# Token scaling for expert dispatch: the 8-token input tile moves to the front, and five of six weight loads move to the load queue

## The chip, the core and the metric

The kernel runs on one core of a Trainium2 chip. The metric is the time of one execution on the device, in microseconds (us); lower is better. The median of six runs is given, and beside it one execution that the hardware profiler recorded.

## What is computed

Each of 16 x 1024 = 16,384 tokens has a row of 512 float32 values, and two expert weights. The output holds, for each token, its row times the first weight and its row times the second:

```python
batch, seq, hidden = x.shape            # 16, 1024, 512
k = expert_indices.shape[-1]            # 2
x_expanded = x[:, :, np.newaxis, :].repeat(k, axis=2)
weights = expert_weights[..., np.newaxis]
return (x_expanded * weights).astype(np.float32)
```

The expert indices are not used for any value. The kernel reads 33.55 MB of input and 0.13 MB of weights, and writes 67.11 MB.

## The kernel before

The 16,384 tokens are dealt to 128 partitions, 128 tokens for each. The list `groups` cuts these 128 into input tiles: five tiles of 24 tokens per partition, then one of 8. A tile of 24 is 48 KB in each partition and 6 MB in all; a tile of 8 is 16 KB and 2 MB. Within a group a partition holds tokens that follow one another in memory, so a tile's load is one contiguous piece per partition.

Three pools hold the data. `w_pool` has one tile with all weights, two per token. `x_pool` has two buffers for input tiles. `o_pool` has two buffers for output tiles, each of `TO` = 12 tokens: 48 KB in each partition, 6 MB in all. An input tile of 24 tokens so becomes two output tiles and two stores; one of 8 tokens becomes one output tile of 32 KB per partition and a store of 4 MB.

There are two queues for transfers. SyncE (SP, the profile's q1) issues the weight loads at the start (line 55), one for each group, and then all stores (line 106). ScalarE (ACT, the profile's q10) issues the input loads (line 76), and computes as well. Each engine works through its instructions in order.

The helper `load(i)` takes an input buffer and issues the load of tile i. Tiles 0 and 1 are loaded ahead of the main loop; the load of tile i + 2 is asked for when tile i's products have been written down, and waits until they are done. In the main loop each token of a tile gives two products of 512 values. Every third product (column `c` of the weights, `c % 3 == 2`) is ScalarE's (line 91), the others are VectorE's (line 97). After each 12 tokens, or at the tile's end, the store is issued.

The framework puts in the waits: a product waits for its input tile, for the weights of its own columns, and for the store that last used its output buffer; a store waits for the products of both engines; a load waits until the products that read its buffer are done. A wait is put on an instruction of the engine that needs it, and what is behind it on this engine waits as well. The framework also decides the order of each engine's instructions, which is close to the order of the source but not always the same: an instruction that stands later in the source can be placed ahead of another that does not depend on it.

Of the kernel before, what the change touches and what calls it, by code (L numbers as in the profile page):

```python
# [1 line left out]

# [4 lines left out]


@with_exitstack
def kernel(  # L10
    ctx: ExitStack,
    tc: tile.TileContext,
    x: bass.AP,
    expert_indices: bass.AP,
    expert_weights: bass.AP,
    out: bass.AP,
):
    nc = tc.nc

    batch, seq, hidden = x.shape  # L20
    k = expert_weights.shape[-1]
    P = nc.NUM_PARTITIONS
    ntok = batch * seq
    assert ntok % P == 0
    A_TOTAL = ntok // P

    f32 = mybir.dt.float32
    row = k * hidden
    TX = 24
    TO = 12  # L30


    groups = [[24], [24], [24], [24], [24], [8]]
    assert sum(sum(g) for g in groups) == A_TOTAL

    xf = x.rearrange("b s h -> (b s) h")
    of = out.rearrange("b s k h -> (b s) (k h)")
    wf = expert_weights.rearrange("b s k -> (b s) k")

    w_pool = ctx.enter_context(tc.tile_pool(name="w_pool", bufs=1))  # L40
    x_pool = ctx.enter_context(tc.tile_pool(name="x_pool", bufs=2))
    o_pool = ctx.enter_context(tc.tile_pool(name="o_pool", bufs=2))

    w_tile = w_pool.tile([P, A_TOTAL * k], f32)

    def rows(of_all, done, T):
        return of_all[done * P : (done + T) * P, :].rearrange(
            "(p a) n -> p (a n)", a=T
        )

    weights = []
    for group in groups:
        weights.append((sum(n for _, n in weights), sum(group)))
    for at, T in weights:
        nc.sync.dma_start(out=w_tile[:, at * k : (at + T) * k], in_=rows(wf, at, T))

    tiles = []
    done = 0
    for group in groups:
        T = sum(group)  # L60
        a0 = 0
        for n in group:
            tiles.append((done, T, a0, n))
            a0 += n
        done += T

    loaded = []

    def load(i):
        if i >= len(tiles):  # L70
            return
        done, T, a0, n = tiles[i]
        x_tile = x_pool.tile([P, TX * hidden], f32)
        cols = rows(xf, done, T)[:, a0 * hidden : (a0 + n) * hidden]
        for lo, hi in [(0, P)]:
            nc.scalar.dma_start(out=x_tile[lo:hi, : n * hidden], in_=cols[lo:hi, :])
        loaded.append(x_tile)

    for i in range(2):
        load(i)  # L80
    for i, (done, T, a0, n) in enumerate(tiles):
        x_tile = loaded[i]
        outr = rows(of, done, T)
        for t in range(n):
            if t % TO == 0:
                o_tile = o_pool.tile([P, TO * row], f32)
            for kk in range(k):
                c = (done + a0 + t) * k + kk
                o = t % TO * row + kk * hidden
                if c % 3 == 2:  # L90
                    nc.scalar.mul(  # L91
                        out=o_tile[:, o : o + hidden],
                        in_=x_tile[:, t * hidden : (t + 1) * hidden],
                        mul=w_tile[:, c : c + 1],
                    )
                    continue
                nc.vector.tensor_scalar(  # L97
                    out=o_tile[:, o : o + hidden],
                    in0=x_tile[:, t * hidden : (t + 1) * hidden],
                    scalar1=w_tile[:, c : c + 1],  # L100
                    scalar2=None,
                    op0=mybir.AluOpType.mult,
                )
            if (t + 1) % TO == 0 or t + 1 == n:
                at = t // TO * TO
                nc.sync.dma_start(  # L106
                    out=outr[:, (a0 + at) * row : (a0 + t + 1) * row],
                    in_=o_tile[:, : (t + 1 - at) * row],
                )
        load(i + 2)  # L110

# [1 line left out]
_INS = ['x', 'expert_indices', 'expert_weights']  # L113
_OUTS = [((16, 1024, 2, 512), 'float32')]


# [23 lines left out]
```

## Time and profile before

| | before |
|---|---|
| median of six runs | 240.81 us (240.47 to 241.04) |
| the profiled execution | 241.0 us |
| its span, first to last instruction | 239.3 us |
| VectorE (DVE) busy | 68.6 us, 171 products of 482 ns |
| ScalarE (ACT) busy | 54.5 us, 85 products of 708 ns and a table load |
| moved by DMA | 100.81 MB, mean 421 GB/s |
| store queue q1 | 65.1% of 16 engines' time |
| load queue q10 | 33.0% |
| first multiply | at 18.51 us |
| stores issued | from 25.02 to 218.81 us, 11 of them |

The 16 DMA engines serve both queues. A transfer of 128 partitions is cut into 128 packets, one for each partition, 8 for each DMA engine, and the trace records when each packet began and how long it took. A share in the table is the sum of the packets' times of a queue over 16 times the span. The span is shorter than the execution's time, since starting and ending the program lies outside it. Times in the views are counted from the start of the span.

VectorE's products start 0.402 us apart where nothing holds them, so the 16 of an output tile take 6.42 us; ScalarE's 8 take 5.01 us beside them. A row of "waits" gives who waited, for what, how long in all, how often, and the longest. The "chain that ended last" is followed back from the last instruction, at each step to what released it.

### The profile page before, as it was taken

Reading aid. Unit: us, or ns where it says so; the run is one execution under the profiler, and the core shown is the slowest. Engines: PE = TensorE matmul, PEld = TensorE weight load, DVE = VectorE, ACT = ScalarE, POOL = GpSimd, SP = SyncE. Lnnn points to the kernel's source line nnn. Section 1 sums busy time; section 2 is a strip of 40 time slices with the busy share of each in tenths; the row PEclk is TensorE's granted clock in tenths of the full one; section 3 lists DMA queues with packets and bytes.
Section 4 is the critical chain, followed back from the end, with each engine's and each line's share of the span. In section 5 each row is a group of like instructions: output and inputs, shape, how many; then the busy total and the mean of one; then the engine's idle time right before and its main releaser. Section 6 shows DMA issues by size and latency. Waiting matters only on the chain.

```text
span 239.3 us, 363 instructions
## 1 busy us (share of the span) xinstructions
DVE 68.6 (29%) x171; ACT 54.5 (23%) x86; POOL 0.2 (0%) x4
## 2 busy tenths in 40 slices
DVE  0009920000370910640064037002805506415000
ACT  0109700000340800620061035002505206213000
POOL 0000000000000000000000000000000000000000
DMA  7999999999999999999999999999999999999894
GB/s 267 462 446 412 412 373 419 485 411 419 460 435 411 437 452 419 411 476 411 427 460 427 403 444 461 411 403 485 419 405 460 408 457 452 403 403 493 383 438 192
DMA packets 3314, 100.81 MB, mean 421 GB/s; under 512 B 1136, under 2 KB 1136, under 8 KB 1136
## 3 DMA queue, kind: packets, MB, share of 16 engines
q1 hardware_dynamic: 2448, 67.24, 65.1%
q10 hardware_dynamic: 864, 33.55, 33.0%
q14 instruction: 2, 0.02, 0.0%
HBM read 33.69 MB, written 67.11 MB: 421 GB/s over the span
## 4 chain that ended last, share of the span: by engine, by line
DMA 60%; DVE 17%; issue 14%; DVEq 0%; SPq 0%
DMA out_dram<-o_tile 53%; DVE o_tile L97 17%; DMA x_tile<-in_x_dram 7%; DVEq L135 0%; DVEq L97 0%; SPq L106 0%
## 5 line engine op out<-in xcount | busy, mean ns | idle before, releaser
L97 DVE TENSOR_SCALAR o_tile<-x_tile,w_tile 128x512 f32<-128x512 f32 x171 | 68.6, 482 | 150.1 <-DMA out_dram<-o_tile 99.2
L91 ACT ACTIVATE o_tile<-x_tile,w_tile 128x512 f32<-128x512 f32 x85 | 53.2, 708 | 157.3 <-DMA out_dram<-o_tile 145.8
L91 ACT ACT_TABLE_LOAD x1 | 1.3, 1283 | 5.7 <-DMA w_tile<-in_expert_weights_dram 5.7
L124 POOL MEMSET const-bfloat16-1.0<- 128x1 bf16 x1 | 0.1, 101 | 0.0
L124 POOL MEMSET const-uint8-127<- 128x1 uint8 x1 | 0.1, 101 | 0.0
L124 POOL MEMSET const-float32-0.0<- 128x1 f32 x1 | 0.1, 98 | 0.2 <-issue 0.2
L124 POOL MEMSET const-float32-1.0<- 128x1 f32 x1 | 0.1, 98 | 0.0
## 6 DMA issues: line engine op xcount, KB each, us to landing
out_dram<-o_tile SPq DMA_DIRECT2D x10, 6144.0 KB, 35.5
x_tile<-in_x_dram ACTq DMA_DIRECT2D x5, 6144.0 KB, 33.2
out_dram<-o_tile SPq DMA_DIRECT2D x1, 4096.0 KB, 19.5
x_tile<-in_x_dram ACTq DMA_DIRECT2D x1, 2048.0 KB, 23.6
w_tile<-in_expert_weights_dram SPq DMA_DIRECT2D x5, 24.0 KB, 31.8
w_tile<-in_expert_weights_dram SPq DMA_DIRECT2D x1, 8.0 KB, 31.2
```

The source lines that it names most:

```text
L91: nc.scalar.mul(out=o_tile[:, o : o + hidden], in_=x_tile[:, t * hidden : (t + 1) * hidden], mul=w_tile[:, c : c + 1],)
L97: nc.vector.tensor_scalar(out=o_tile[:, o : o + hidden], in0=x_tile[:, t * hidden : (t + 1) * hidden], scalar1=w_tile[:, c : c + 1], scala ...
L124: nc = _bacc.Bacc("TRN2", target_bir_lowering=False, num_devices=1)
```

## The change

The list of groups begins with the 8-token tile, and the five of 24 come behind it. Only the weights of the first group are still loaded by SyncE, ahead of its stores. ScalarE issues the other five weight loads, between the load of the first input tile and that of the second. The number of products, stores and loads, and their sizes, are the same. The tile of 8 tokens and its 4 MB store are now the first and not the last.

```diff
-    groups = [[24], [24], [24], [24], [24], [8]]
+    groups = [[8], [24], [24], [24], [24], [24]]
...
-    for at, T in weights:
-        nc.sync.dma_start(out=w_tile[:, at * k : (at + T) * k], in_=rows(wf, at, T))
+
+    def load_weights(queue, part):
+        for at, T in part:
+            queue.dma_start(out=w_tile[:, at * k : (at + T) * k], in_=rows(wf, at, T))
+
+    load_weights(nc.sync, weights[:1])
...
-    for i in range(2):
-        load(i)
+    load(0)
+    load_weights(nc.scalar, weights[1:])
+    load(1)
```

In the changed kernel the lines are numbered a little higher: the weight loads are line 57, the input loads line 80, ScalarE's products line 96, VectorE's line 102 and the stores line 111. In the built order, ScalarE's instructions before were: two loads, the 16 products of the first tile, the third load, the products of the second tile. After, they are: the 8-token load, five weight loads, the second tile's load, the 5 products of the first tile, one product of the second tile, the third load, the other products of the second tile.

## The prediction

> **What bounds the kernel now.** I read the page's slices first, then the queues, the chain and the waits, the windows, and last the records of single packets in the trace.
>
> ```profile
> DMA  7999999999999999999999999999999999999894
> q1 hardware_dynamic: 2448, 67.24, 65.1%
> q10 hardware_dynamic: 864, 33.55, 33.0%
> ```
>
> The first line is the busy share of the 16 DMA engines in 40 slices of 6 us: it is at its top from the second slice to the last but two. The next two are the store queue (SP, q1) and the load queue (ACT, q10): together 98.1% of the span. Nothing else is near its limit: VectorE is busy 29% and ScalarE 23%.
>
> ```profile
> 0.72 17.77 DMA x_tile<-in_x_dram
> 18.51 6.44 DVE o_tile L97 x16
> 188.80 25.38 DMA out_dram<-o_tile
> DVE o_tile L97 <- DMA x_tile<-in_x_dram: 18.5, 1, 18.5
> ACT o_tile L91 <- DMA out_dram<-o_tile: 145.8, 9, 35.1
> ```
>
> The first three are pieces of the chain (start, length, what), the others rows of the waits. The multiplies stand idle for 18.5 us at the start, until the first input tile has landed, and after that they wait for stores to give back output buffers. Neither idle time is idle time of the transfers, as the windows show (length; DVE, ACT and POOL busy; clock; DMA share; GB/s):
>
> ```profile
> 5.40:29.70 24.30, 11.19 (x29) 11.20 (x17) 0.00 (x0) 1.00 0.98 422
> 29.70:32.30 2.60, 1.58 (x4) 0.00 (x0) 0.00 (x0) 1.00 1.03 304
> 34.20:63.50 29.30, 0.00 (x0) 0.00 (x0) 0.00 (x0) 1.00 1.00 431
> 218.80:235.90 17.10, 0.00 (x0) 0.00 (x0) 0.00 (x0) 1.00 1.00 432
> ```
>
> So the end is set by how much the transfers have to move and by what they lose, hardly by when a multiply runs. The packet records give the sum. A 48 KB packet takes 1.815 us, a 32 KB one 1.213 and a 16 KB one 0.611; every transfer of 128 partitions gives each engine 8 packets. Loads: five of 8 x 1.815 and one of 8 x 0.611, 77.5 us. Stores: ten of 8 x 1.815 and one of 8 x 1.213, 154.9 us. That is 232.4 us for each engine. The first packet starts at 1.72, the last ends at 238.0, the span is 239.3, and this execution took 241.0: 1.7 outside the span. The median shown is 240.81, so 0.2 comes off at the end.
>
> The loss beside the 232.4 is small and can be placed. Packets that took longer than their size's usual time add 0.58 us per engine in the first 5 us, 0.84 between 29 and 32.2 us, and 0.21 in all the rest. All sixteen packets of the second group are an engine's last packet of the second input tile, and right behind each come weight packets:
>
> ```profile
> DMA packets 544, 1.64 MB, mean 364 GB/s; under 512 B 512, under 2 KB 512, under 8 KB 512
> w_tile<-in_expert_weights_dram SPq DMA_DIRECT2D x5, 24.0 KB, 31.8
> ```
>
> The first line is of the stretch 29.7 to 34.2 us: 512 small packets. The second says that weights on the store queue take 31.8 us to land. The records show why: with both queues filled, an engine takes one packet of each in turn, so one weight packet goes out with every 1.8 us of input.
>
> **The change part by part.** *The small tile in front.* In the first trace the first multiply starts at 18.51. The tile's eight packets per engine now take 0.611 instead of 1.815, so it starts at 18.51 - 8 x 1.204 = 8.9 us. Its 16 products take 4.44 us (the row of the last, 8-token tile), the first store (4 MB) is issued at 13.4 and, with the 1.0 us from issue (0.72) to first packet (1.72), moves from 14.4. Before it was issued at 25.02 and moved from 32.6. That is 18 us earlier, but the engines were moving input then, which has to be moved anyway: bytes and packet sizes are the same, only in another order. Worth nothing by itself.
>
> *The large tile at the end.* The last store is 6 MB instead of 4. The three last stores run back to back. An output buffer comes back 0.5 us after its store has landed, its multiplies take 6.44, the issue 0.05 and the first packet 1.0: 8.0 us, under the 14.5 us of the other buffer's store, which covers it. The stretch from the last packet's end to the span's end stays 1.3 us. Nothing again; uncovered, it would cost 8.0 each time.
>
> *The load of the third tile.* The built order has one more move that the diff doesn't show. Before, ScalarE issued this load behind the last product of the first tile. Now it stands behind the first product of the second tile, which waits for that tile to land. Behind this wait stand the load itself and 7 more products. Does the load queue's gap show? The second tile starts per engine at about 9.6 (first tile landed at 8.5, and about 1.2 for the weights, below). Three packets go out by 15.0, the other five alternate with the first store: 5 x (1.815 + 1.213) = 15.1, so it lands at 30.1. Then 0.4 to the product, 0.7 for it, 1.0 for issue to packet: the third tile moves from 32.2. The first store has three packets left at 30.1, that is 3.6 us, to 33.7. Covered by 1.5 us. The next store follows at 30.5 + 6.44 + 1.05 = 38.0, while the load runs. Zero, with a thin cover; without it 2.1 us.
>
> Here a rule of the Trainium skill speaks against the change. "DMA: Bandwidth & Descriptors", section "Queues, rings and completion order", has an engine drain a whole packet, some 9 to 17 descriptors, of one queue before it turns to another. By that the first store's eight would go at one turn, be done before the tile lands, and the gap of 2.1 us would be open. The records here alternate one by one (20 and 20 large packets of the two queues between 35 and 40 us), so I go by the row.
>
> *The weights in the load queue.* Each of the five transfers is 8 packets per engine and one 4-byte packet that signals the end: 45. Before, 15 of them went out between input packets at 0.016 us, 0.24 in all; 30 went in one run at a pitch of 0.0117, 0.35; and the packet before that run was stretched by 0.84. Removed: 1.43 us. Now all 45 stand in one run between the first and second tile, with nothing on the other queue: 45 x 0.0117 = 0.53, plus a stretch that this trace doesn't show. Bounds: nothing, if reading ahead hides it as it hid the 15 (sum 0.53, change -0.9); in proportion to the run above, 0.84 x 45/30 = 1.26 (sum 1.79, +0.4); at the rate of the start, where 9 small packets stand beside a stretch of 0.58, 0.58/9 x 45 = 2.9 (sum 3.4, +2.0). I take 1.26, from the nearest row: a run of the same packets right behind input. ScalarE issues the five at about 0.45 us each, so the second load is issued at about 4 us, before the first tile has moved: no cost; uncovered it would be 5 x 0.45 = 2.3 us. The first weights stay alone on SP; they land before the first tile as now (the table load, released by them, starts at 5.75).
>
> The same page, "Anatomy of one DMA", gives a fixed cost of about 2.0 us for each DMA issued by GpSimd, and its rules call transfers under 64 KB mostly overhead. Five in a row at that price would be 10 us and the total 249. On one engine the records have the ends of three such transfers at 32.34, 32.44 and 32.54: 0.1 us apart, so they don't wait for one another.
>
> Sum: 241.0 + 0.4 = 241.4 in the frame of the profiled execution, 241.2 as a median.
>
> **The rivals.** *Cheap run.* The stretch vanishes: 240.8 - 0.9 = 239.9. For it: the 15 interleaved packets cost their 0.016 and no stretch. Against it: both runs of small packets in this trace stand beside stretched ones. Chance 0.2.
>
> *Dear run, slower.* The price per small packet at the start holds: 240.8 + 2.0 = 242.8. It decides when the last packets of the first tile, 0.611 us each, are too short to hide the reading of 45 small pieces which 1.815 us half hid. For it: the cover is a third as long. Against it: the stretch at the start may be the first access and not the weights. Chance 0.2.
>
> *Dry queue.* The third tile's load comes after the first store has run out; up to 2.1 us on all engines, 242.3 to 242.9. It decides when the store has at most one packet left as the tile lands, that is when it starts less than two input packets after the tile. Chance 0.08.
>
> *It does what an earlier start suggests.* The multiplies begin 9.6 us sooner, and all of it shows: 231.2. Against it: 232.4 us of packets, 1.7 before, 1.3 behind and 1.7 outside are 237.1 already. Chance 0.02.
>
> **How the numbers follow.** The forecast, 241.2, has 0.5; its own range is 240.4 to 241.9, from a stretch that stays at 0.84 whatever the number, less the 0.3 by which runs differ, to the sum and as much again. About 0.2% (0.48 us) is what can be told from no change, so 240.33 to 241.29 counts as the same. Faster: the cheap run nearly whole, the last rival and a little of the forecast, 0.22. Slower: the dear run, most of the dry queue and a quarter of the forecast, 0.38. The same: 0.40. The range for 8 in 10 goes from the cheap run's 239.8 to the dear one's 242.9.
>
> **What would show it.** Right: a DMA share of 1.0 from about 10 us on; first multiply near 8.9; first store issued near 13.4; stretched input packets around 7 to 9 us, with about 1.8 us between the last first-tile packet at its usual time and the first large one of the second; the third load issued at about 31 with no lower DMA share at 30 to 34. Wrong: a dip in the share at any later place, a last packet that ends more than 2 us from 238.4, or a stretch of the engines' last packets in another place.

## The result, and the profile after

| | before | after |
|---|---|---|
| median | 240.95 us (41 runs) | 242.29 us (19 runs) |
| ratio, with its 95% interval | | 1.0056 [1.0044, 1.0067] |
| the profiled execution | 241.0 us | 242.94 us, a second one 241.65 us |
| its span | 239.3 us | 241.3 us, the second 240.0 us |

The changed kernel is slower by 1.3 us, 0.56%. It scatters more: 241.2 to 243.56 us, against 240.47 to 241.96. The first profile of it lies 0.65 us above its median and the second as far below.

The page's busy slices of the 16 DMA engines and the two queues, after:

```profile
DMA  6999999999999999999999999999999999999991
...
q1 hardware_dynamic: 1728, 67.12, 64.3%
q10 hardware_dynamic: 1584, 33.68, 33.2%
```

The bound is the same: 97.5% of the span is packets. The load queue now has the weights' packets, 720 more. Pieces of the chain (start, length, what):

```profile
4.22 25.35 DMA x_tile<-in_x_dram
...
29.66 6.44 DVE o_tile L102 x16
...
36.15 34.26 DMA out_dram<-o_tile
```

and rows of the waits (who waited for what: us in total, times, longest):

```profile
ACT o_tile L96 <- DMA out_dram<-o_tile: 136.7, 9, 29.2
...
DVE o_tile L102 <- DMA x_tile<-in_x_dram: 25.2, 2, 16.0
```

Both engines wait for inputs twice now, 9.2 and 16.0 us on VectorE, and for stores as before. The chain runs through the second tile's load, which lands at 29.6, and then through the second store, issued at 36.15. The timeline (start, length, engine, line, what) shows what stands between the two:

```profile
9.18 4.45 DVE L102 TENSOR_SCALAR o_tile<-x_tile,w_tile 128x512 f32<-128x512 f32 x11 [9.18 <-DMA x_tile<-in_x_dram]
...
29.65 0.72 ACT L96 ACTIVATE o_tile<-x_tile,w_tile 128x512 f32<-128x512 f32 x1 [17.30 <-DMA x_tile<-in_x_dram]
29.73 0.33 ACTq L80 DMA_DIRECT2D x_tile<-in_x_dram  x1
...
36.25 5.01 ACT L96 ACTIVATE o_tile<-x_tile,w_tile 128x512 f32<-128x512 f32 x8 [1.59 <-DMA out_dram<-o_tile]
```

ScalarE's single product of the second tile waits 17.30 us for that tile, and the third load, behind it, goes out at 29.73. The last row says that the first store had landed by 36.25, at about the moment that the second was issued. So the store queue had nothing to move until then, and another 3.9 us pass from that issue to a first packet. The DMA view of 33.6 to 37.6 us (queue, kind: packets, MB, share) says it directly:

```profile
q10 hardware_dynamic: 33, 1.62, 93.9%
q1 hardware_dynamic: 6, 0.00, 0.1%
```

Six store-queue packets in 4 us, all of them 4-byte ends of a transfer. The packet records put the first store's last packets at 32.8 to 34.0 us and the second store's first ones at 40.1 to 41.8. On one engine that is a pause of 7.3 us between two store packets, in which it moves four load packets. The engines were not idle: the third load ran alone. The loss therefore has to be sought in the packets themselves. Time beyond the usual for a packet's size, in us per engine, in both profiles of each kernel (packets sorted by when they began):

| began at | before | before, second | after | after, second |
|---|---|---|---|---|
| 0 to 7 us | 0.58 | 0.46 | 0.44 | 0.51 |
| 7 to 33 us | 0.84 | 0.77 | 0.65 | 0.11 |
| 33 to 60 us | 0.00 | 0.00 | 0.47 | 0.73 |
| 60 us to the end | 0.21 | 0.18 | 0.36 | 0.07 |
| mean end of the 16 engines | 236.53 | 236.45 | 237.11 | 236.74 |
| last end | 238.01 | 238.11 | 239.94 | 238.66 |

The mean engine of the first profile ends 0.58 us later, the last one 1.93. The execution ends with the last. The row of 33 to 60 us is new: it is nothing before the change, and it begins where the store queue starts again. In the second profile a smaller second row makes up for it: summed over the whole execution the stretches are 1.63 and 1.41 us before, 1.92 and 1.42 after. What sets both profiles of the changed kernel apart is how unevenly the engines end: the last is 1.48 and 1.66 us behind the mean before, 2.83 and 1.92 after. The stretches of 33 to 60 us fall unevenly: two engines in the first profile and three in the second have load packets stretched one after the other, some 4 us apart, between 35 and 54 us. The records don't name an engine. I joined packets to chains by their times, and an engine's own share is less sure than the means and the last end.

### The profile page after: what moved, and what is told of

Read it like the earlier page. It is cut to its first block, busy times and chain, and to the rows that moved or that the text cites. A ratio compares the mean times of both kernels' runs of the same rounds, so it can differ in the third digit from the quotient of the medians.

```text
span 241.3 us, 364 instructions
## 1 busy us (share of the span) xinstructions
DVE 68.7 (28%) x171; ACT 54.6 (23%) x86; POOL 0.2 (0%) x4
## 4 chain that ended last, share of the span: by engine, by line
DMA 65%; DVE 16%; another core or an unknown queue 7%; ACTq 1%; issue 1%; DVEq 0%; SPq 0%
DMA out_dram<-o_tile 55%; DVE o_tile L102 16%; DMA x_tile<-in_x_dram 11%; ACTq L57 1%; ACTq L80 0%; DVEq L140 0%; DVEq L102 0%; SPq L111 0%
```

## The experiments

Each run has its own runs of the kernel before beside it on the same chip, and ratios are against these. Edits are shown against the changed kernel where nothing else is said. The first four take the change apart.

**Order alone** (all six weight loads on the store queue):

```diff
-    load_weights(nc.sync, weights[:1])
+    load_weights(nc.sync, weights)
...
-    load_weights(nc.scalar, weights[1:])
```

> The tiles are in the changed order (8 tokens in front), all six weight loads are on the store queue as before. Theory W (the five weight loads in the load queue cost the 1.35 us): back to 240.9 to 241.2, ratio 0.999 to 1.001. Theory O (the order: with the small tile in front the store queue runs empty once after its first store, at 33 to 40 us, and each start of stores stretches load packets): still slower, 241.9 to 242.7, ratio 1.004 to 1.007. Both: a stretched input packet per engine just ahead of its first store packet, 0.6 to 0.85 us on average, if the stretch belongs to the first store; if it belongs to runs of weight packets, it stands where those are.

240.84 us, ratio 0.9989 [0.9968, 1.0010]: not slower. It has the 8-token tile in front and the late third load (issued at 24.41). But the first store waits in its queue behind the weights, whose packets go out one for each input packet: it is issued at 13.49 and moves from 23 us. So it lasts to 38 or 41 us. The second store is issued at 30.84, so the store queue never runs out; 0.05 us of stretched packets at 33 to 60 us. Theory W foretold the time, and as the next but one shows for another reason.

**Weights alone** (the old order of tiles):

```diff
-    groups = [[8], [24], [24], [24], [24], [24]]
+    groups = [[24], [24], [24], [24], [24], [8]]
```

> The tiles are in the old order, the five later weight loads are in the load queue between the first two input tiles. Theory W: 241.9 to 242.7, ratio 1.004 to 1.007. Theory O: as before, 240.5 to 241.2, ratio 0.998 to 1.001. If the stretch of 0.84 us ahead of the first store belonged to the weights, it moves to about 17 us; if to the first store, it stays just ahead of the first store packet, which now can start sooner since nothing is queued before it on the store queue.

240.70 us, 0.9975 [0.9962, 0.9988]. Moving the weights costs nothing; Theory W is refuted here. The stretched packets begin at 26.7 to 31.6 us (0.60 in all), just ahead of the first store's first packets at 28.9 to 31.7, with no weight packet near: these went out from 17.0 to 18.7 us.

**The change without its five later weight loads:**

```diff
-    load_weights(nc.scalar, weights[1:])
...
-                        mul=w_tile[:, c : c + 1],
+                        mul=w_tile[:, c % 16 : c % 16 + 1],
```

(and the same column for VectorE's products)

> The changed kernel without its five later weight loads; all products use the first tile's weight columns, so the output is not the reference's. Theory W: the whole difference goes, 240.2 to 241.0, ratio 0.997 to 1.000. Theory O: only the run of small packets goes, about 0.5 us, 241.4 to 242.0, ratio 1.002 to 1.005.

242.18 us, 1.0032 [1.0013, 1.0051]. Without any weights in the load queue it is still slower. The store queue is empty as long as in the change (7.6 us between two of its large packets on one engine, 7.3 there), and 0.49 us per engine is stretched at 33 to 60 us. So each half of the change alone is harmless, and the harm needs no weights in the load queue: it needs them out of the store queue, where they held the first store back.

**Tiles of 20, four of 24, and 12:**

```diff
-    groups = [[8], [24], [24], [24], [24], [24]]
+    groups = [[20], [24], [24], [24], [24], [12]]
```

> The changed kernel with tiles of 20, four of 24 and one of 12 tokens: the weights are placed as in the change, but two stores are queued from the first tile, so the store queue does not run empty at 33 to 40 us. Theory W: 241.9 to 242.7, ratio 1.004 to 1.007. Theory O: 240.6 to 241.3, ratio 0.999 to 1.002, and no stretched load packets at 35 to 55 us.

241.07 us, 0.9993 [0.9979, 1.0007], and 0.01 us stretched at 33 to 60. As Theory O says; but the first store also starts later (26.8 us), so an early first store could still be the cost. The next runs separate the two.

**The second tile in two loads of 12:**

```diff
-    groups = [[8], [24], [24], [24], [24], [24]]
+    groups = [[8], [12, 12], [24], [24], [24], [24]]
```

> The changed kernel with its second tile loaded as two tiles of 12 tokens: the 8-token tile in front, the weights in the load queue and the early first store (packets from about 17 us) stay, but the second store is ready some 10 us sooner, before the first has left the store queue. Theory R (the cost is the start of stores after the store queue ran empty, at about 40 us): ratio 0.998 to 1.001, no stretched load packets at 35 to 55 us, the last engine ends within 2 us of the mean. Rival E (an early first store is itself the cost): ratio 1.003 to 1.007 as in the change.

244.19 us, 1.0120 [1.0090, 1.0149]: neither theory's number. My design was wrong: the gap moved. The windows (length; DVE, ACT, POOL; clock; DMA share; GB/s):

```profile
48.00:54.00 6.00, 1.24 (x4) 0.00 (x0) 0.00 (x0) 1.00 1.01 385
75.00:80.00 5.00, 2.12 (x6) 2.17 (x4) 0.00 (x0) 1.00 0.88 315
80.00:90.00 10.00, 10.00 (x26) 7.74 (x13) 0.00 (x0) 1.00 0.90 335
```

The store queue now starts again twice, at 53 to 55 and at 88 to 91 us. The rate is low in front of both starts; the stretches are 0.88 us per engine at 33 to 60 us and 2.15 behind 60, on all engines. Around 78 us both queues were empty too, so not all of the 3 us is stretch. It fits Theory R but doesn't decide it.

**Tiles of 12, four of 24, and 20:** One size changed:

```diff
-    groups = [[8], [24], [24], [24], [24], [24]]
+    groups = [[12], [24], [24], [24], [24], [20]]
```

> The changed kernel with 12 tokens in the first tile and 20 in the last: the first store is 6 MB and lasts until the second is queued. Theory R: ratio 0.998 to 1.001, no second start of the store queue, no stretched packets at 35 to 55 us. Rival E: the first store moves from about 22 us, still 10 us earlier than before, so ratio 1.002 to 1.005.

240.56 us, 0.9983 [0.9968, 0.9997]. The first store moves from 22 to 25 us, lasts to 42 to 45, and the second follows. 0.03 us stretched at 33 to 60 us.

**Tiles of 10, four of 24, and 22:**

```diff
-    groups = [[8], [24], [24], [24], [24], [24]]
+    groups = [[10], [24], [24], [24], [24], [22]]
```

> The changed kernel with 10 tokens in the first tile and 22 in the last. The first store starts nearly as early as in the change (packets from 19 to 21 us against 17.5 to 20) but is 5 MB, and by the sum of its packets and those of the loads beside it lasts to about 41 us, where the second store's packets begin (38 to 40). Theory R (the store queue runs empty and starts again): no or a very short empty stretch, ratio 0.998 to 1.001, under 0.1 us of stretched packets per engine at 33 to 60 us. Rival E (the early first store costs): ratio 1.002 to 1.006.

240.66 us, 0.9986 [0.9977, 0.9996], with two tokens more in front than the change. First store from 20.9 to 22.3 us, a little later than foretold; no gap, nothing stretched at 33 to 60 us. The first store's own start is beside 1.08 us of stretch per engine, the most of any kernel, and it is not slower.

**The third load first.** The change, with an order edge that puts the third load ahead of ScalarE's products of the second tile's first half:

```diff
                 if c % 3 == 2:
-                    nc.scalar.mul(
+                    with tc.issue_after(last.ins) if i == 1 and t < TO else ExitStack():
+                        nc.scalar.mul(
...
-        load(i + 2)
+        last = load(i + 2)
```

(the helper returns its load)

> The changed kernel with one more edit: the third tile's load stands ahead of ScalarE's first product of the second tile, as it did before the change, so it is issued at about 14 us and not at 29. The first store's packets then alternate with this load after 29 us and last to about 40 us instead of 33. Everything else, the early first store too, is as in the change. Theory R: no empty store queue at 33 to 40 us, ratio 0.998 to 1.001, under 0.1 us of stretched packets per engine at 33 to 60 us. Rival E: ratio 1.003 to 1.007.

240.72 us, 0.9994 [0.9976, 1.0013]. This decides between the two. Tiles, weights and the early first store (from 17.6 to 18.7 us) are those of the change. Its timeline (the row of the store is from the view of 27 to 45 us):

```profile
13.61 0.37 ACTq L80 DMA_DIRECT2D x_tile<-in_x_dram  x1
...
29.52 6.42 DVE L104 TENSOR_SCALAR o_tile<-x_tile,w_tile 128x512 f32<-128x512 f32 x16 [16.00 <-DMA x_tile<-in_x_dram]
36.01 0.33 SPq L113 DMA_DIRECT2D out_dram<-o_tile  x1
41.45 5.01 ACT L98 ACTIVATE o_tile<-x_tile,w_tile 128x512 f32<-128x512 f32 x8 [6.94 <-DMA out_dram<-o_tile]
```

and its DMA view of 33.6 to 37.6 us:

```profile
q1 hardware_dynamic: 30, 0.98, 56.9%
q10 hardware_dynamic: 16, 0.79, 45.4%
```

The load goes out at 13.61 and not at 29.73. The products behind the first store's buffer start *later*, at 41.45 and not 36.25, because the store shares the engines with the load. But the second store is issued at 36.01, before the first one's last packets end at 38.2 to 39.3 us, so the store queue never runs out of work (30 of its packets in those 4 us, large ones, against 6 small). No store packet moves from 39.3 to 41.8 us even so: each engine moves two load packets between the two stores, where in the change it moves four. Nothing is stretched at 33 to 60 us, and the time is that of before. Rival E is refuted.

The edit also brings the third load forward, so the late load itself, or its empty queue, could have been the cost. Earlier runs rule that out. With 10 tokens in front this load stands behind the same single product and is issued later than in the change, at 30.99. The DMA view of 29 to 35 us there shows the load queue without a large packet:

```profile
q1 hardware_dynamic: 63, 2.58, 99.4%
q10 hardware_dynamic: 16, 0.00, 0.1%
```

The second store is issued at 37.42, before the first ends at 38.5 to 41.7, and that kernel is not slower. Nor is the one with 12 tokens in front, whose third load is issued at 32.66. What these kernels share with the edit is a store queue that doesn't run out.

**The kernel before without its five later weight loads:**

```diff
-    for at, T in weights:
+    for at, T in weights[:1]:
```

(products take columns modulo 48)

> The kernel before without its five later weight loads; all products use the first tile's weight columns, so the output is not the reference's. If the stretch of 0.84 us ahead of the first store belonged to the weight packets, as the prediction had it: 1.4 us less, ratio 0.994, and no stretch at 25 to 32 us. If it belongs to the first start of stores: only the packets themselves go, 0.4 to 0.7 us, ratio 0.997 to 0.999, and the stretch of 0.5 to 0.85 us per engine stays just ahead of the first store packet.

240.39 us, 0.9967 [0.9956, 0.9979]: 0.8 us less. The stretch ahead of the first store is still there, 1.01 us per engine at 7 to 33 us. It is not the weights'.

**The change once more, unedited:**

> The changed kernel once more, for a second profile of it. Theory R: the store queue starts again at about 40 us on every engine, stretched load packets of 0.4 to 0.5 us per engine on average between 35 and 55 us, and at least one engine ends 2 us or more behind the mean; all of it would be absent or elsewhere if the first profile's stretches were chance.

The profile is the second column of "after" above. The second start is at 39.8 to 41.0 us on every engine, with 0.73 us stretched at 33 to 60 (more than the 0.4 to 0.5 foretold) and the last engine 1.9 us behind the mean, just under the 2 us foretold. The first store's start, at 17.4 to 18.1 us, this time has only 0.11 beside it: the stretch at a start is not the same each time.

**The weights alone once more,** the edit as above:

> The kernel with only the weights moved, once more, since it was the fastest that computes everything. If its gain is real: ratio 0.996 to 0.999, the interval below 1. If it was chance: an interval that holds 1. The weights' packets leave the store queue, so the first store's packets can start about 3 us sooner than before the change, which by itself moves no byte sooner; so a gain would have to be in stretched packets or in how unevenly the 16 engines end.

240.75 us, 0.9982 [0.9970, 0.9995].

**The kernel before, unedited,** as a control:

> The kernel before against itself, to see what a ratio of no change looks like: 0.999 to 1.001, the interval around 1. A second profile of it: no stretched packets at 33 to 60 us, and one stretched load packet per engine ahead of its first store packet.

240.92 us, 0.9990 [0.9979, 1.0001]. The kernel before against itself is thus 0.1% off. Against that, the weights-only version's 0.9975 and 0.9982 are a gain of about 0.1 to 0.15%, 0.2 to 0.4 us, and 10 or 12 tokens in front are within its reach. The control's interval overlaps all of theirs. These versions beat the changed kernel clearly and the kernel before hardly.

## Why the prediction was right, and where its steps were not

The range, 239.8 to 242.9 us, holds 242.29, and the sign of the small forecast (+0.4 us, against +1.3 measured) was the right one. The forecast's own range, 240.4 to 241.9, doesn't hold it: the wide one does because of its upper part, which came from the dear run, and that did not happen. So the hit is in good part luck. Two terms of the sum were wrong in opposite directions, and the mechanism that made the loss is one that the text priced at zero.

*What bounds the kernel*: right. The share of packets is above 97% in both kernels, and 9.3 us won on the first product (at 9.18; 8.9 foretold) brought nothing by itself.

*First store*: issued at 13.70 as foretold (13.4), but its packets began at 17.5 to 20.0, not at 14.4. The 1.0 us from issue to first packet was measured where the engines stood idle. Beside a running load queue some two more load packets go out first, 3.6 us.

*The weights in the load queue*: the step that failed. The 45 packets per engine did go out at the pitch foretold, between 7.2 and 9.2 us, so 0.53 us; but the stretch of 1.26 us that was added to them is zero. The stretched input packets foretold for 7 to 9 us are missing; they begin at 15.0 to 19.4 us and then from 33 us on. In this the run behaved like the "cheap run" rival. And the 0.84 us that the sum took off together with the weights belongs to the first store: it stands ahead of it in nearly every kernel whose first store starts beside a running load, without weights too (1.01 us). I had put it down to the small packets because they were its neighbours in the records; the other neighbour, the first store, came right behind them and was overlooked. So the term of +0.4 is about zero: the weights' packets take 0.53 us against 0.59 before, and the weights moved alone gave 0.9975 and 0.9982.

*The third load*: the step that missed the loss. The text found the moved load, saw that it would wait for the second tile, and asked whether the engines would run dry. By the sum's thin cover they would not, and it wrote zero. They didn't, but there was no cover left: the load's first packets came 3.1 us or more after its issue, not 1.0, at 32.8 to 34.0 us, just as each engine finished the first store. The gap of the store queue was even in the numbers: the first store out at 33.7, the next at 38.0. The true ones are 33 and 40. What was not asked is what an empty *store queue* costs while loads run on: with the load put back in front, the ratio goes from 1.0056 to 0.9994, 1.5 us. With the load in front the mean engine ends at 236.36 us and the last at 237.77; in the two profiles of the change the mean is 0.75 and 0.38 later and the last 2.17 and 0.89. The stretches behind the second start mark the place, but their sum over the whole execution doesn't tell slow from fast: 1.92 and 1.42 us in the change, 0.90 to 1.74 in the versions that are not slower. How far the last engine is behind the mean does: 2.83 and 1.92 us, and 2.38 without the five weight loads, against 0.98 to 1.66.

*The other rivals*: "dry queue" named the right place, the third load behind the second tile, with the wrong mechanism: it wanted the first store gone and both queues empty. Its 2.1 us were not paid in the change, where the load's packets followed the store's without a gap. "Dear run" had a time near the result, 242.8, and no part in it. That the earlier start would show in full was ruled out rightly by the sum of packets.

*The rules of the Trainium skill*: that an engine drains a whole packet, typically 9 to 17 descriptors, of one queue before it turns ("DMA: Bandwidth & Descriptors", "Queues, rings and completion order") would have let the first store run ahead of the second tile. The runs don't show that: beside the loads the large packets alternate, and the first store ends at 32.8 to 34.0 us, after the tile has landed at 29.6. The fixed cost of about 2.0 us on the same page ("Anatomy of one DMA") is stated for DMAs that GpSimd issues. ScalarE issued the five weight loads, so no run here tests it, and five times that price isn't seen: the five are through in 2 us together.

What stays open: why a start of stores beside running loads stretches the loads' packets, how a pause of the store queue makes some engines end so late, and why the first start costs no time on balance (1.08 us of it in the kernel with 10 tokens in front, which is among the fastest) while the second does. The later stretches on single engines, 4 us apart, suggest that engines which fall behind the others stay at a disadvantage. That is argued, not shown.

## What to carry to other kernels

Where transfers bound a kernel, look at each queue by itself and not only at the engines' busy share: here the share stayed near 1.0 while one queue's packets on an engine were 7.3 us apart, and each version that kept this queue supplied lost nothing. A change that lets one stream start earlier can make it run out before its next piece is ready, and something that only seemed in the way (weights ahead of the first store) may have been keeping the streams in step. Compare the built order of each queue, since a load that slides behind one waiting product moved 16 us here without a line of the diff saying so.

## What was not expected of the hardware

- A store issued beside a running load stream moved its first packet on an engine 3.8 to 6.3 us after its issue (13.70 to 17.5 and 20.0), against 1.0 us from idle for the first transfer of the kernel (0.72 to 1.72).
- The load packets just ahead of a first store packet take longer by 0.1 to 1.1 us per engine on average, in kernels with and without weights near.
- 45 small packets, 40 of 192 bytes and 5 of 4, pass an engine in 0.53 us, one every 11.7 ns, behind a load and ahead of another, with no packet beside them stretched (the change, 7.2 to 9.2 us).
